# A hybrid decoder step: chunks of a half wait in the order for products sent, L in two buffers, X filled by memsets

## The chip, the cores and the metric

One core of a Trainium2 chip runs the whole step as one program. The metric is the time of one execution on the device, in microseconds. The engines of the core work side by side, each in the order in which its instructions were written out: TensorE (PE, with its weight loads PEld), VectorE (DVE), ScalarE (ACT), GpSimd (POOL) and SyncE (SP), which here only issues DMAs. POOL issues DMAs too.

## The reference

A layer of a decoder for 1024 tokens of a prompt and 8 samples of 4 tokens (T = 1056 columns). A wide projection feeds a causal convolution branch and an RWKV-7 branch, and two gates merge them; a gated MLP with a short convolution follows.

```python
h = rmsnorm(x, norm_mix_g)
z = h @ w_in                     # conv | r, k, v, lora | gates
u = zc[..., :D_CONV] * jax.nn.sigmoid(zc[..., D_CONV:])
c, new_conv = causal_dwconv(conv_buf, u, conv_dw_w, conv_dw_b)
ya = jax.nn.silu(layernorm(c, ...)) @ w_conv_out
# RWKV-7: S_t = S_{t-1} diag(w_t) + (S_{t-1} a_t) b_t^T + v_t k_t^T ;  y_t = S_t r_t
yh, new_wkv = wkv7_scan(wkv_state, rh, decay, kh, -kk, kk * ah, vh)
yb = ((groupnorm(yh) + bonus) * gout) @ w_rw_out
m = gates[..., :D_MODEL] * ya + gates[..., D_MODEL:] * yb
x = x + m @ w_mix_out
up = rmsnorm(x, norm_ffn_g) @ w_up
cu, new_ffn = causal_dwconv(ffn_buf, up, ffn_dw_w, ffn_dw_b)
x = x + (jax.nn.gelu(cu[..., :D_FF]) * cu[..., D_FF:]) @ w_down
```

## The kernel before

Every large product is done with split operands: a weight tile of 128 columns is loaded (`wraw`), rounded on ACT (`whi`, L48) and its rest taken on DVE (`wlo`, L49), and three matmuls (high by high, high by low, low by high) of 352 columns are summed in PSUM (tile `mm`, written at L54). A tile of 128 output rows is 3 blocks of 8 x 3 = 72 such matmuls.

`mixer_a` does the convolution input, the LoRA parts and the first six tiles of k, r and v. `mixer_b` does the recurrence and, between its steps, other products. The recurrence is cut into 16 halves n of 4 heads and 256 tokens (J = n // 4 counts the group of heads, n % 4 the place in the sequence). Each half goes through:

- `prep` and `operands`: loads k, r, v and others from DRAM, scales them, writes E and BK. A half of group J needs the k, r and v tiles 2J and 2J + 1 (`s_prep` waits for "rkv").
- `stage`: products of BK and E, whose PSUM tiles DVE evicts into LQ (L1024, L1028); the diagonal blocks of 32 go to DRAM (`dL`, L1038) and come back as `L` with one lane per partition, four times over (L1040). A triangular **solve** on DVE follows: `X` is set to the identity (L1043), and 31 pairs of a multiplication into `tm` (L1047) and an addition into `X` (L1049) build the inverse. `X` goes to DRAM (`dX`, L1051) and back into LQ (L1055).
- `combine`: two transposes on DVE (L1085) and 32 small matmuls complete the inverse.
- `chain`: 4 chunks of 64 tokens, one after the other, since each needs the state that the one before leaves. A chunk has three steps of four matmuls into a tile `c`; after each DVE (and ACT) must answer: `R0` (L1143), `UV` (L1151), `UV` or `Sf` (L1162). ACT takes the result out of tile `y` at the end (`Yev`, L1173).
- `group_norm`, and beside it the samples' work (`s_samples`) and the layer norm of the convolution (`s_ln`).

Other products stand between: 18 tiles of k, r and v (`rkv_tile`, j from 2 to 7), 16 gates (`gate`) and 8 tiles of the convolution's output (`conv_out`, 36 matmuls each). They come from the generator `fillers`. The loop `drive` writes the program: it holds a clock that counts matmul columns, takes a step of the first stream whose time has come, and one filler matmul group when none has. A stream that waits for something undone looks again every 400 units. So this loop sets in which order work is written; the tile framework then orders each engine's instructions once more by its own plan. In `fillers`, k, r and v tiles come first; then gates as far as `due` allows: the first GATE0 = 5 freely, and gate number g + 5 only when chain g is written. `conv_out` waits for the last chain and for `ln`; its input tile lies where the halves' E, BK, LQ and UV lay (`conv_in`). Behind it come `merge`, `mix` and the MLP (`tail`).

Of the kernel before, what the change touches and what calls it, by code (L numbers as in the profile page):

```python
# [31 lines left out]
class Net:  # L32
# [587 lines left out]
    def wkv_consts(self):  # L620
        nc, cp = self.nc, self.cp

        self.mb = cp.tile([128, 8, 32], F32, name="mb")
        nc.vector.memset(self.mb, 0.0)
        self.mrow = cp.tile([128, 8], F32, name="mrow")
        self.ms = cp.tile([128, 2, 32], F32, name="ms")
        nc.vector.memset(self.mrow, 1.0)
        nc.vector.memset(self.ms, 1.0)
        for b in range(8):
            nc.vector.memset(self.mb[:, b, 4 * b:4 * b + 4], 1.0)  # L630
        for p in range(4):
            r = self.mrow[32 * p:32 * (p + 1)]

            nc.gpsimd.affine_select(out=r, in_=r, pattern=[[-4, 8]], compare_op=ALU.is_ge, fill=0.0, base=0, channel_multiplier=1)
            nc.gpsimd.affine_select(out=r, in_=r, pattern=[[4, 8]], compare_op=ALU.is_ge, fill=0.0, base=3, channel_multiplier=-1)
            m = self.ms[32 * p:32 * (p + 1)]
            for q in range(2):
                x = m[:, q]
                nc.gpsimd.affine_select(out=x, in_=x, pattern=[[1, 32]], compare_op=ALU.is_ge, fill=0.0,
                                        base=-1 + q, channel_multiplier=-1)  # L640
                nc.gpsimd.tensor_tensor(
                    out=x.rearrange("p (b t) -> p b t", t=4), in0=x.rearrange("p (b t) -> p b t", t=4),
                    in1=r.rearrange("p (b o) -> p b o", o=1).to_broadcast([32, 8, 4]), op=ALU.mult)

        self.x0 = cp.tile([128, 8, 32], F32, name="x0")
        nc.vector.memset(self.x0, 0.0)
        for q in range(4):
            x = self.x0[32 * q:32 * (q + 1)]
            nc.gpsimd.affine_select(out=x, in_=x, pattern=[[4, 8], [-1, 32]], compare_op=ALU.not_equal, fill=1.0,
                                    base=q, channel_multiplier=0)  # L650

        self.tri = cp.tile([128, 2, 64], F32, name="tri")
        nc.vector.memset(self.tri, 1.0)
        for x in range(2):
            w = self.tri[64 * x:64 * x + 64]
            nc.gpsimd.affine_select(out=w, in_=w, pattern=[[1, 2], [1, 64]], compare_op=ALU.is_ge, fill=0.0,
                                    base=-1, channel_multiplier=-1)
        self.bt = cp.tile([128, 128], F32, name="bt")
        nc.vector.memset(self.bt, 0.0)
# [21 lines left out]
    def mixer_b(self):  # L681
        nc, a = self.nc, self.a
        self.wkv_consts()
        self.t2_left = self.T2N
        self.want = 0
        self.t_stage = {}
        self.st, self.pr, self.ch = {}, {}, {}
        with ExitStack() as e:
            self.t4 = self.pool(e, "t4b", 3)
            self.t2 = self.pool(e, "t2", self.T2N)  # L690
            self.e_sg = ExitStack()
            self.sg = self.pool(self.e_sg, "stage", 3, side="right")
            self.ln = self.pool(e, "lanes", 1)
            self.sm = self.pool(e, "small", 2)
            sp = self.pool(e, "samples")
            self.sG, self.sQK = (sp.tile([128, 4, 64], F32, name=x) for x in ("sG", "sQK"))
            self.sbv = sp.tile([128, 4, 32], F32, name="sbv")
            self.sUV = sp.tile([128, 8, 64], F32, name="sUV")
            self.sPC = sp.tile([128, 8, 8], F32, name="sPC")
            dram = lambda nm, m, w: [self.dr.tile([m, w], F32, name=f"{nm}{i}") for i in range(ND)]  # L700
            self.d_BT, self.d_S = dram("d_BT", 64, 128), dram("d_S", 128, 512)
            self.d_bv = [self.dr.tile([128, 2, TP], F32, name=f"d_bv{i}") for i in range(ND // 2)]
            self.drive([self.s_chain(), self.s_comb(), self.s_stage(), self.s_norm(), self.s_prep(), self.s_samples(), self.s_ln(), self.s_y(), self.s_shift()],
                       self.fillers())
            self.e_sg.close()
# [44 lines left out]
    def s_chain(self):  # L750
        for n in range(self.NH):
            yield from self.wait(("comb", n))
            yield from self.chain(n)
            self.done.add(("chain", n))

# [23 lines left out]
    def s_prep(self):  # L779
        for n in range(self.NH):  # L780
            k = [("rkv", j, x) for j in (n // 4 * 2, n // 4 * 2 + 1) for x in range(3)]
            if n == 8 + self.SQ[2]:
                k.append(("steps", 0))
            yield from self.wait(*k)
            yield from self.take(8, 2)
            yield from self.prep(n)
            yield from self.wait(*([("chain", n - 3)] if n > 2 else []))
            self.operands(n)
            self.done.add(("prep", n))

    def s_samples(self):
        def one(g, n):
            yield from self.take(n)
            yield from g
            self.t2_left += n
        for g in range(2):
            for j in range(4 * g, 4 * g + 4):
                yield from self.wait(("prep", j // 2 * 4 + self.SQ[j // 2]))
                yield from one(self.samples_in(j), 4)
                if g:  # L800
                    yield from one(self.samples_state(j - 4), 3)
            yield from one(self.samples_steps(4 * g), 4)
            self.done.add(("steps", g))
        for j in range(4, 8):
            yield from one(self.samples_state(j), 3)
# [47 lines left out]
            self.t2_left += 1  # L853
            yield 5000

    GATE0 = 5

    def fillers(self):
        gates = [(i, x) for x in range(2) for i in range(ND)]
        due = lambda: len(gates) > 2 * ND - self.GATE0 or ("chain", 2 * ND - len(gates) - self.GATE0) in self.done  # L860
        tiles = [(j, x) for j in range(2, ND) for x in range(3)]
        conv = list(range(ND))
        loaded = False
        while gates or tiles or conv:
            if not loaded and ("chain", self.NH - 1) in self.done and "ln" in self.done:
                self.conv_in()
                loaded = True
            if tiles:
                yield from self.rkv_tile(*tiles.pop(0))
            elif gates and due():  # L870
                yield from self.gate(*gates.pop(0))
                if not gates:
                    self.done.add("gates")
            elif conv and loaded:
                yield from self.conv_out(conv.pop(0))
            else:
                yield 1
# [17 lines left out]
    def prep(self, n):  # L895
# [32 lines left out]
        nc.scalar.activation(out=t1, in_=kn, func=AF.Square)  # L928
        hs = [slice(0, 64), slice(64, 128)]
        if smp:  # L930
            ARs = self.sm.tile([128, 2, 2, 32], F32, tag="ARs", name="ARs")
            BKs = self.sm.tile([128, 2, 2, 32], F32, tag="BKs", name="BKs")
            vs = self.sm.tile([128, 2, 32], F32, tag="vs", name="vs")
            bt4 = lambda t: t.rearrange("p u (b t) -> p u b t", t=4)
            nc.gpsimd.tensor_tensor(out=bt4(ARs[:, :, 0]), in0=sp(kn), in1=PS_[:, :, :, 0:4], op=ALU.mult)
            nc.gpsimd.tensor_tensor(out=bt4(ARs[:, :, 1]), in0=sp(r), in1=PS_[:, :, :, 1:5], op=ALU.mult)
            nc.gpsimd.tensor_copy(out=vs, in_=v[:, :, 256:288])
# [73 lines left out]
    def stage(self, n):  # L1011
# [24 lines left out]
        for x in range(2):  # L1036
            for d in range(2):
                nc.sync.dma_start(out=dL[x, d].rearrange("c i j -> i c j"), in_=LQ[64 * x + 32 * d:64 * x + 32 * d + 32, :, 32 * d:32 * d + 32])  # L1038
        L = self.ln.tile([128, 32, 32], F32, tag="L", name="L")
        nc.sync.dma_start(out=L, in_=dL.rearrange("(o h) d c i j -> o (h d c) (i j)", o=1).to_broadcast([4, 32, 1024]))  # L1040
        X = self.ln.tile([128, 8, 32], F32, tag="X", name="X")
        tm = self.ln.tile([128, 80], F32, tag="tm", name="tm")
        nc.vector.tensor_copy(out=X, in_=self.x0)  # L1043
        for s in range(31):
            a, m = s // 4 + 1, 31 - s
            tp = tm[:, :a * m].rearrange("p (a m) -> p a m", m=m)
            nc.vector.tensor_tensor(out=tp, in0=L[:, s:s + 1, s + 1:32].to_broadcast([128, a, m]),  # L1047
                                    in1=X[:, :a, s:s + 1].to_broadcast([128, a, m]), op=ALU.mult)
            nc.vector.tensor_tensor(out=X[:, :a, s + 1:32], in0=X[:, :a, s + 1:32], in1=tp, op=ALU.add)  # L1049
        for q in range(4):  # L1050
# [650 lines left out]
```

## Time and profile before

| | |
|---|---|
| median of 3 runs | 2529.82 us (2526.34 to 2546.9) |
| the profiled execution | 2521.95 us, span 2520.3 us |
| mean granted clock of TensorE | 0.928 of 2.4 GHz |
| PE busy | 2341.8 us (93%) |
| DVE busy | 1646.8 us (65%) |
| ACT busy | 877.9 us (35%) |
| POOL busy | 263.2 us (10%) |
| DMA | 230.65 MB, mean 92 GB/s |

The span is the profiled execution from its first instruction to its last. A share of busy time is an average over stages with different limits; a busy PE is not a PE at its peak, since ends of matmuls are modelled. The granted clock has two levels, 1.2 and 2.4 GHz, and a number between them is a mean over a stretch.

### The profile page before, as it was taken

What the parts mean: (1) busy time and instruction counts of PE and PEld (TensorE: products, weight loads), DVE (VectorE), ACT (ScalarE), POOL (GpSimd) and SP (SyncE); (2) the same over time, 40 slices, a digit from 0 to 9 for tenths busy, and PEclk for the clock granted to TensorE, in tenths of its full rate; (3) what the DMA queues carried; (4) which work ended last, traced back from release to release, by engine and by line L of the source; (5) the groups of instructions that cost most, each with busy time, mean ns of one, the idle gap of its engine ahead of it and who ended that gap; (6) DMA issues with size and microseconds to landing.
All of it is one profiled execution on the core that took longest, in us unless ns stands there. A gap on an engine that the chain in (4) does not pass through costs nothing.

```text
span 2520.3 us, 41895 instructions
## 1 busy us (share of the span) xinstructions
PE 2341.8 (93%) x16094; PEld 2114.6 (84%) x16094; DVE 1646.8 (65%) x4190; ACT 877.9 (35%) x1748; POOL 263.2 (10%) x562
## 2 busy tenths in 40 slices
PE   6789998987889689889999999999999999999998
PEld 5778886765668567767879999999999999999998
DVE  5999777688787877786862344475555545545556
ACT  4234333344344433543443222333232322223235
POOL 2313311011111111221221100000000000000000
PEclk9989997867679789897999999999999999999999
DMA  4124543243323332434334654431111111111111
GB/s 124 49 75 147 172 131 98 55 108 86 107 58 100 107 106 78 125 85 107 106 83 148 234 167 132 122 125 44 46 41 54 35 51 46 45 48 44 51 52 70
DMA packets 289295, 230.65 MB, mean 92 GB/s; under 512 B 82333, under 2 KB 265271, under 8 KB 288575
## 3 DMA queue, kind: packets, MB, share of 16 engines
q1 hardware_dynamic: 268615, 170.17, 24.3%
q0 software_dynamic: 20480, 57.80, 6.6%
q8 instruction: 127, 2.08, 0.4%
q14 instruction: 73, 0.60, 0.1%
HBM read 157.45 MB, written 70.45 MB: 90 GB/s over the span
## 4 chain that ended last, share of the span: by engine, by line
PE 78%; DVE 12%; DMA 6%; ACT 2%; issue 2%; SPq 1%; DVEq 0%; ACTq 0%; POOLq 0%
PE mm L54 62%; PE w L54 6%; PE c L54 2%; PE y L54 2%; DMA L<-dL 2%; DVE sg L359 2%; PE w L61 2%; DMA dX<-X 2%; DVE X L1049 1%; DVE tm L1047 1%; DVE wlo L49 1%; DMA d_ma<-ga 0%; SPq L1051 0%; DVE E L1030 0%; DVE UV L1162 0%
## 5 line engine op out<-in xcount | busy, mean ns | idle before, releaser
L54 PE MATMUL mm<-hH,whi 128*128 128x352 f32 (+1 forms) x2568 | 875.9, 341 | 14.1 <-DVE bcol L497 12.7
L54 PE MATMUL mm<-hH,wlo 128*128 128x352 f32 (+1 forms) x2568 | 851.9, 333 | 18.6 <-DVE wlo L49 18.6
L54 PE MATMUL mm<-hL,whi 128*128 128x352 f32 (+1 forms) x2568 | 854.2, 333 | 0.2 <-DVE hL L248 0.2
L54 PEld LDWEIGHTS mm<-hH,whi 128*128 128x128 f32 (+1 forms) x2568 | 491.2, 191 | 42.8 <-DVE bcol L497 14.3
L54 PEld LDWEIGHTS mm<-hH,wlo 128*128 128x128 f32 (+1 forms) x2568 | 491.6, 192 | 30.8 <-DVE wlo L49 20.8
L54 PEld LDWEIGHTS mm<-hL,whi 128*128 128x128 f32 (+1 forms) x2568 | 492.6, 192 | 11.0 <-issue 2.2
L48 ACT ACTIVATE whi<-wraw 128x1024 fp32r<-128x1024 f32 (+2 forms) x123 | 126.1, 1025 | 425.6 <-PE mm L54 340.3
L1533 DVE TENSOR_TENSOR u<-mm,rs 128x352 f32<-128x352 f32 x144 | 73.5, 511 | 225.1 <-PE mm L54 225.0
L49 DVE TENSOR_TENSOR wlo<-wraw,whi 128x1024 fp32r<-128x1024 f32 (+2 forms) x123 | 145.4, 1182 | 91.5 <-ACT whi L48 91.4
L359 DVE SCALAR_TENSOR_TENSOR sg<-cu,par,sg 128x1024 f32<-128x1024 f32 x120 | 165.4, 1382 | 1.5
L54 PE MATMUL mm<-fH,whi 128*128 128x352 f32 x504 | 163.4, 324 | 0.0
L54 PE MATMUL mm<-fH,wlo 128*128 128x352 f32 x504 | 162.8, 323 | 0.0
L54 PE MATMUL mm<-fL,whi 128*128 128x352 f32 x504 | 162.7, 323 | 0.0
L1588 DVE TENSOR_TENSOR acc<-mm,acc 128x352 f32<-128x352 f32 x168 | 86.9, 522 | 93.6 <-PE mm L54 93.6
L1563 DVE SCALAR_TENSOR_TENSOR c<-u,par,c 128x1024 f32<-128x1024 f32 x96 | 122.9, 1280 | 7.7 <-ACT c L1559 5.3
L54 PE MATMUL w<-E,BK 64*128 64x128 f32 x512 | 93.2, 332 | 32.4 <-DVE tm L1047 13.1
L54 PEld LDWEIGHTS w<-E,BK 64*128 64x128 f32 x512 | 76.5, 227 | 49.4 <-issue 27.3
L1047 DVE TENSOR_TENSOR tm<-L,X 128x60 f32<-128x60 f32 (+24 forms) x496 | 100.4, 202 | 23.6 <-DMA L<-dL 18.4
L1049 DVE TENSOR_TENSOR X<-X,tm 128x60 f32<-128x60 f32 (+24 forms) x496 | 100.4, 202 | 5.3
L54 PEld LDWEIGHTS mm<-fH,whi 128*128 128x128 f32 x504 | 94.8, 188 | 0.5
L54 PEld LDWEIGHTS mm<-fH,wlo 128*128 128x128 f32 x504 | 95.0, 188 | 0.0
L1122 ACT ACTIVATE SP<-UV,PC 64x64 f32<-64x64 f32 x192 | 64.3, 343 | 87.9 <-DVE UV L1162 78.0
(404 smaller groups left out, 3663.5 us busy)
## 6 DMA issues: line engine op xcount, KB each, us to landing
wraw<-w_in SPq DMA_DIRECT2D x50, 512.0 KB
wraw<-w_up SPq DMA_DIRECT2D x48, 512.0 KB
wraw<-w_down SPq DMA_DIRECT2D x32, 384.0 KB
L<-dL SPq DMA_DIRECT2D x16, 512.0 KB
d_alr<-la POOLq DMA_DIRECT2D x8, 528.0 KB, 3.2
d_cum<-lc POOLq DMA_DIRECT2D x8, 528.0 KB, 3.5
d_gout<-lg POOLq DMA_DIRECT2D x8, 528.0 KB, 4.0
d_k<-k POOLq DMA_DIRECT2D x24, 176.0 KB, 2.9
```

The lines of the kernel that those rows point to most:

```text
L48: nc.scalar.activation(out=hi[:, :nk, :m], in_=raw[:, :nk, :m], func=AF.Copy)
L49: (lo_eng or nc.vector).tensor_tensor(out=lo[:, :nk, :m], in0=raw[:, :nk, :m], in1=hi[:, :nk, :m].bitcast(F32), op=ALU.subtract)
L54: self.nc.tensor.matmul(out, l, r, start=start, stop=stop)
L61: self.nc.tensor.transpose(out, x, ident)
L359: nc.vector.scalar_tensor_tensor(out=c[:, 0:TP], in0=u[:, t:t + TP], scalar=self.col("conv_w", t * 4 + i), in1=c[:, 0:TP], op0=ALU.mult, o ...
L1047: nc.vector.tensor_tensor(out=tp, in0=L[:, s:s + 1, s + 1:32].to_broadcast([128, a, m]), in1=X[:, :a, s:s + 1].to_broadcast([128, a, m]), ...
L1049: nc.vector.tensor_tensor(out=X[:, :a, s + 1:32], in0=X[:, :a, s + 1:32], in1=tp, op=ALU.add)
L1122: nc.scalar.activation(out=at(SP, u, x), in_=src(x)[:, u], func=AF.Copy, scale=PC[hs[x], 4 * u + c:4 * u + c + 1])
L1533: nc.vector.tensor_tensor(out=u[:, 2 + t0:2 + t0 + m], in0=p, in1=rs[:, t0:t0 + m], op=ALU.mult)
L1563: nc.vector.scalar_tensor_tensor(out=c[:, 0:TP], in0=u[:, t:t + TP], scalar=wt, in1=c[:, 0:TP], op0=ALU.mult, op1=ALU.add)
L1588: nc.vector.tensor_tensor(out=acc[i][:, s], in0=ps[:, :BW], in1=acc[i][:, s], op=ALU.add)
```

## The change

Five edits go together:

1. `s_chain` counts: before half n's chain is written, 4 + 2n filler tiles (at most 34, which is all 18 of k, r and v and all 16 gates) must have been written. `fillers` counts them in `filled`.
2. GATE0 is 16, so gates wait for no chain.
3. `L` (one buffer of 4 KB a partition) is replaced by `LT` (rows 0 to 15 of the block, 2 KB) and `LB` (the lower right quarter, 1 KB), each with two buffers. LT comes in one DMA, LB in four.
4. `X` is set by five memsets on POOL instead of a copy on DVE from a constant `x0`, which is dropped.
5. `ARs`, `BKs` and `vs` have one buffer instead of two, and the `prep` that writes them waits for the samples of the group before ("samples").

```diff
-        self.x0 = cp.tile([128, 8, 32], F32, name="x0")
...
     def s_chain(self):
         for n in range(self.NH):
             yield from self.wait(("comb", n))
+            while self.filled < min(self.FILL[0] + self.FILL[1] * n, 34):
+                yield self.POLL
             yield from self.chain(n)
...
+            if n // 4 and n % 4 == self.SQ[n // 4]:
+                k.append(("samples", 2 * (n // 4) - 1))
...
                 yield from one(self.samples_in(j), 4)
+                self.done.add(("samples", j))
...
-    GATE0 = 5
+    GATE0 = 16
+    FILL = (4, 2.0)
...
             if tiles:
                 yield from self.rkv_tile(*tiles.pop(0))
+                self.filled += 1
             elif gates and due():
                 yield from self.gate(*gates.pop(0))
+                self.filled += 1
...
-            ARs = self.sm.tile([128, 2, 2, 32], F32, tag="ARs", name="ARs")
+            ARs = self.sm.tile([128, 2, 2, 32], F32, tag="ARs", name="ARs", bufs=1)
...
-        L = self.ln.tile([128, 32, 32], F32, tag="L", name="L")
-        nc.sync.dma_start(out=L, in_=dL.rearrange("(o h) d c i j -> o (h d c) (i j)", o=1).to_broadcast([4, 32, 1024]))
+
+        LT = self.ln.tile([128, 16, 32], F32, tag="LT", name="LT", bufs=2)
+        LB = self.ln.tile([128, 16, 16], F32, tag="LB", name="LB", bufs=2)
+        lanes = dL.rearrange("h d c i j -> (h d c) i j")
+        nc.sync.dma_start(out=LT, in_=lanes[:, 0:16].rearrange("(o l) i j -> o l (i j)", o=1).to_broadcast([4, 32, 512]))
+        for q in range(4):
+            nc.sync.dma_start(out=LB[32 * q:32 * q + 32], in_=lanes[:, 16:32, 16:32])
         X = self.ln.tile([128, 8, 32], F32, tag="X", name="X")
         tm = self.ln.tile([128, 80], F32, tag="tm", name="tm")
-        nc.vector.tensor_copy(out=X, in_=self.x0)
+        nc.gpsimd.memset(X, 0.0)
+        for q in range(4):
+            nc.gpsimd.memset(X[32 * q:32 * q + 32].rearrange("p a t -> p (a t)")[:, q:256:36], 1.0)
         for s in range(31):
             a, m = s // 4 + 1, 31 - s
             tp = tm[:, :a * m].rearrange("p (a m) -> p a m", m=m)
-            nc.vector.tensor_tensor(out=tp, in0=L[:, s:s + 1, s + 1:32].to_broadcast([128, a, m]),
+            nc.vector.tensor_tensor(out=tp, in0=(LT[:, s:s + 1, s + 1:32] if s < 16 else LB[:, s - 16:s - 15, s - 15:16]).to_broadcast([128, a, m]),
                                     in1=X[:, :a, s:s + 1].to_broadcast([128, a, m]), op=ALU.mult)
```

What edits 1 and 2 do to the engines' order shows at the last chain. On PE before, this piece is from the last half's chain (`c` and `y` are its matmuls, `mm<-hH` and `mm<-hL` those of a gate):

```order
L54 MATMUL c<-R_13195,LQ 64x64 x4
L54 MATMUL mm<-hH,wlo 128x352
L54 MATMUL mm<-hH,whi 128x352
L54 MATMUL mm<-hL,whi 128x352
L54 MATMUL y<-UV,LQ 64x64
L54 MATMUL mm<-hH,wlo 128x352
L54 MATMUL c<-UV,BK 64x64 x4
L54 MATMUL y<-UV,LQ 64x64 x3
```

After the change, the end of the last chain on PE, up to the first matmul of `conv_out` (`mm<-csH`):

```order
L54 MATMUL c<-R_14305,LQ 64x64 x4
L54 MATMUL y<-UV,LQ 64x64
L54 MATMUL c<-UV,BK 64x64 x4
L54 MATMUL y<-UV,LQ 64x64 x3
L61 MATMUL w<-ident,Sf 64x128 x2
L54 MATMUL mm<-csH,whi 128x352
L54 MATMUL mm<-csL,whi 128x352
```

The products of gates that stood between the steps, and those that followed the chain, now stand ahead of it, between the steps of earlier chains.

On DVE before, the start of half 9's solve: `X<-x` sets X, `tm<-L,X` and `X<-X,tm` are the solve, and `LQ<-w` are evictions of half 10's stage, from which half 10's L is made:

```order
L1043 COPY X<-x_2805 128x256
L1024 TENSOR_TENSOR LQ<-w,nin 64x4x64
L1028 TENSOR_TENSOR LQ<-w,tri 64x4x64
L1030 TENSOR_TENSOR E_8806<-w,tri 64x512
L1047 TENSOR_TENSOR tm<-L,X 128x31
L1024 TENSOR_TENSOR LQ<-w,nin 64x4x64
L1049 TENSOR_TENSOR X<-X,tm 128x31
L1028 TENSOR_TENSOR LQ<-w,tri 64x4x64
L1047 TENSOR_TENSOR tm<-L,X 128x30
```

After the change, evictions of half 9's stage on DVE, between the solves of halves 8 and 9; the first multiplication of half 9's solve stands 24 rows behind the last of these rows:

```order
L1026 TENSOR_TENSOR LQ<-w,nin 64x4x64
L669 SCALAR_TENSOR_TENSOR ry<-rt,ry 128x8
L1030 TENSOR_TENSOR LQ<-w,tri 64x4x64
L1251 TENSOR_TENSOR Yev<-Yev,ry 128x512
L1032 TENSOR_TENSOR E_8681<-w,tri 64x512
L941 TENSOR_TENSOR alr<-alr,k 128x576
L1026 TENSOR_TENSOR LQ<-w,nin 64x4x64
L1030 TENSOR_TENSOR LQ<-w,tri 64x4x64
L1032 TENSOR_TENSOR E_8682<-w,tri 64x512
```

The stage's evictions moved from within the solve before to behind it, and the copy into X is gone from DVE. X is set on POOL now, here between the memsets of the same stage's LQ:

```order
L1197 DMA out_p_wkv<-so 64x4x64
L1029 MEMSET LQ 32x4x32 x2
L1050 MEMSET X 128x256
L1052 MEMSET X 32x8 x4
L1029 MEMSET LQ 32x4x32
L506 DMA d_r_485<-r 128x352
```

The two rows that write X were added; before, the memsets of LQ and the DMA issues stood without them.

## Rows read from the trace of the kernel before

**Rows 1.** Page, chain that ended last: shares of the span by engine.
```profile
PE 78%; DVE 12%; DMA 6%; ACT 2%; issue 2%; SPq 1%; DVEq 0%; ACTq 0%; POOLq 0%
```

**Rows 2.** Stretches: length, busy of PE, PEld, DVE, ACT, POOL (instructions), clock, DMA, GB/s.
```profile
1453.00:2520.00 1067.00, 1059.22 (x6595) 1040.23 (x6594) 578.45 (x998) 314.17 (x541) 21.50 (x81) 1.00 0.23 68
...
340.00:1321.00 981.00, 858.99 (x7034) 686.86 (x7033) 740.31 (x2710) 392.49 (x922) 137.22 (x301) 0.83 0.35 93
...
1321.00:1453.00 132.00, 127.70 (x792) 126.54 (x790) 45.54 (x72) 37.56 (x56) 16.41 (x30) 0.99 0.59 194
...
567.00:767.00 200.00, 160.82 (x1403) 128.75 (x1402) 162.91 (x644) 79.79 (x193) 21.38 (x48) 0.72 0.32 88
767.00:855.00 88.00, 81.60 (x715) 66.27 (x713) 63.37 (x197) 44.41 (x103) 11.39 (x25) 0.98 0.35 103
...
1092.00:1280.00 188.00, 176.98 (x1478) 139.20 (x1479) 144.18 (x531) 73.27 (x176) 38.33 (x76) 0.90 0.38 104
...
1197.00:1323.00 126.00, 125.53 (x1175) 97.99 (x1175) 90.62 (x335) 55.72 (x132) 26.01 (x46) 1.00 0.36 94
...
1280.00:1321.00 41.00, 41.00 (x392) 30.27 (x393) 21.36 (x63) 17.70 (x42) 6.01 (x10) 1.00 0.27 65
```

**Rows 3.** Stretches, the solve's additions (L1049) alone: length, DVE busy (instructions), clock.
```profile
767.00:855.00 88.00, 0.00 (x0) 0.98 0.35 103
...
1052.00:1092.00 40.00, 0.00 (x0) 0.89 0.47 116
```

**Rows 4.** Stretches, tile mm alone: length, busy of PE, PEld, DVE, ACT, clock.
```profile
340.00:1321.00 981.00, 428.41 (x1839) 317.41 (x1840) 40.53 (x134) 39.94 (x77) 0.83 0.35 93
567.00:767.00 200.00, 61.32 (x255) 47.56 (x256) 8.37 (x28) 5.54 (x10) 0.72 0.32 88
767.00:855.00 88.00, 53.36 (x249) 39.33 (x247) 7.23 (x24) 6.08 (x11) 0.98 0.35 103
1092.00:1280.00 188.00, 95.39 (x411) 68.39 (x412) 0.00 (x0) 8.24 (x18) 0.90 0.38 104
1197.00:1323.00 126.00, 76.65 (x336) 53.16 (x337) 0.00 (x0) 6.48 (x14) 1.00 0.36 94
1321.00:1453.00 132.00, 126.68 (x778) 125.29 (x778) 11.83 (x24) 9.60 (x21) 0.99 0.59 194
1333.00:1401.00 68.00, 68.00 (x430) 68.00 (x428) 0.00 (x0) 8.25 (x18) 1.00 0.35 106
```

**Rows 5.** Waits of DVE, 340 to 1321 us: total, times, longest.
```profile
DVE R L1143 <- PE c L54: 41.6, 29, 5.5
...
DVE tm L1047 <- DMA L<-dL: 18.4, 6, 6.1
```

**Rows 6.** Timeline of DVE: start, duration, line, operation; half 0's solve ends, 1's begins.
```profile
405.81 0.15 DVE L1049 TENSOR_TENSOR X<-X,tm 128x8 f32<-128x8 f32 x1
...
413.09 1.22 DVE L49 TENSOR_TENSOR wlo<-wraw,whi 128x1024 fp32r<-128x1024 f32 x1
414.22 0.28 DVE L1043 COPY X<-x 128x256 f32<-128x256 f32 x1
...
418.54 0.19 DVE L1047 TENSOR_TENSOR tm<-L,X 128x31 f32<-128x31 f32 x1 [0.71 <-DMA L<-dL]
```

**Rows 7.** Chain that ended last, behind the last half: start, duration, work.
```profile
1321.14 4.98 DMA cs<-d_cs
...
1331.82 66.18 PE mm L54 x416
```

**Rows 8.** Chain that ended last: landings of L and of dX.
```profile
408.04 10.41 DMA L<-dL
...
509.85 8.69 DMA dX<-X
```

**Rows 9.** Groups of POOL, 340 to 1321 us: busy, mean ns, idle before and its enders.
```profile
L1027 POOL MEMSET LQ<- 32x128 f32 x64 | 12.7, 199 | 179.0 <-DVE LQ L1024 158.1 <-DVE tm L1047 14.0 <-issue 5.3
```

**Rows 10.** Timeline of SP: start, duration, four issues of dX.
```profile
405.99 2.00 SPq L1051 DMA_DIRECT2D dX<-X  x4
```

More of the change, by code (lines that the diff above doesn't have):

```diff
@@ L643, in wkv_consts @@
                     in1=r.rearrange("p (b o) -> p b o", o=1).to_broadcast([32, 8, 4]), op=ALU.mult)
-        self.x0 = cp.tile([128, 8, 32], F32, name="x0")
[L646 to L650, printed above, removed]
         self.tri = cp.tile([128, 2, 64], F32, name="tri")
@@ L686, in mixer_b @@
         self.t_stage = {}
+        self.filled = 0
         self.st, self.pr, self.ch = {}, {}, {}
@@ L930, in prep @@
         if smp:
-            ARs = self.sm.tile([128, 2, 2, 32], F32, tag="ARs", name="ARs")
-            BKs = self.sm.tile([128, 2, 2, 32], F32, tag="BKs", name="BKs")
-            vs = self.sm.tile([128, 2, 32], F32, tag="vs", name="vs")
+            ARs = self.sm.tile([128, 2, 2, 32], F32, tag="ARs", name="ARs", bufs=1)
+            BKs = self.sm.tile([128, 2, 2, 32], F32, tag="BKs", name="BKs", bufs=1)
+            vs = self.sm.tile([128, 2, 32], F32, tag="vs", name="vs", bufs=1)
             bt4 = lambda t: t.rearrange("p u (b t) -> p u b t", t=4)
```

## Prediction

> **What bounds the kernel now.** I read the chain that ended last first: PE holds 78% of it, DVE 12%, DMA 6% [rows 1]. So TensorE's order decides, and the question is where it is not dense. The windows answer that [rows 2]: from 1453 us on PE is busy 1059.22 of 1067 us at clock 1.00, and nothing can be won there. The mixer's second half, from 340 to 1321 us (the 16 halves with their solves and chains), takes 981 us with PE busy 858.99, DVE 740.31 and a mean clock of 0.83. It is followed by 132 us (1321 to 1453) that are dense again.
>
> Three things are wrong with the 981 us. First, they hold only 1839 of the products named mm, while 778 more stand behind them [rows 4]; 8 conv tiles of 36 make 288 of those, so 490 gate products (6.8 tiles of 72) run alone after the last chain. Second, no half is solved in two stretches, 767 to 855 us and 1052 to 1092 us: the count of the solve's additions there is zero [rows 3]. An ordinary turn from one solve to the next took 12.7 us (405.81 to 418.54) [rows 6], so 88 + 40 - 2 x 12.7 = 103 us are lost. Halves 8 and 12 need k, r and v tiles that the order sends late: before, chains run ahead of them and then wait. Third, the clock follows the density of products: 255 of them in 200 us go with clock 0.72, 411 in 188 us with 0.90, 249 in 88 us with 0.98 [rows 2, 4].
>
> **What one matmul costs.** A dense stretch gives 68.00 us / 430 = 0.158 us for a product [rows 4]. From 1197 to 1323 us PE is busy 125.53 of 126 us at clock 1.00 with 336 products among 1175 matmuls [rows 2, 4]; the other 839 (chains, stages, transposes) are then worth (126 - 336 x 0.158) / 839 = 0.087 us each. At these prices the 981 us hold 1839 x 0.158 + 5195 x 0.087 = 742 us of work: PE is used to 0.76. The last stretch of four solves, 1092 to 1280 us, holds 411 products and 1067 others, 158 of 188 us: 0.84. The stretch 767 to 855 holds 249 and 466: 80 of 88 us, 0.91.
>
> **The order (GATE0, FILL), the stage.** After the change all 34 tiles stand before the end of the last chain, 1839 + 490 = 2329 products in the stage, two tiles ahead of each half; the last tile that half 8 needs is the 12th and that of half 12 the 18th, which chains 4 and 7 already wait for, and the two empty stretches have no reason left. The order also moves the solves: on DVE the rows between the last row of a solve and the first step of its own chain grow from a mean of 50 to 162 (over all 16), so a chain no longer waits for the transfers between them. PE work becomes 2329 x 0.158 + 5195 x 0.087 = 820 us. Below that the stage can't go; at the 0.84 of the last stretch it takes 976 us. DVE gains 7 splits of weights, 740.31 + 7 x 1.22 = 749 us (a split took 1.22 us) [rows 2, 6]; at the 0.815 of its densest stretch (162.91 of 200 us) [rows 2] it needs 919 us. I take 915 us, where PE would be used to 0.90, between the two stretches above: **-66 us**, with ends -5 and -161.
>
> **The last chain runs bare.** In the new order no product stands between its steps; what hid its latency is gone. Today the end, 1280 to 1321 us, is 41 us at clock 1.00 with PE full [rows 2]. By the prices, the matmuls alone are cheaper without the products, but a chain step waits for DVE and back (DVE waited 41.6 us in 29 times for the first product of a chunk, longest 5.5) [rows 5]. Between nothing and 15 us more than PE's use allows for, I take **+8 us**.
>
> **Behind the chain.** The 490 products leave: 132 us shrink to what remains. conv_in must wait for the chain's buffers, and after it 1331.82 - 1321.14 = 10.7 us pass until PE goes on with products that need it not; the load, the split and the subtraction end about there [rows 7]. Gates cover this today; then it is open. Conv keeps what lies between the end of the run of gates and the merge, 1453 - (1331.82 + 66.18) = 55 us, its stalls included. So 132 becomes 66: **-66 us**.
>
> **L, X.** Waits for the load of L cost DVE 18.4 us in 6 times, 3.1 us each [rows 5]. Two buffers let the load start earlier, but the new order sends stage evictions later: fewer than 35 DVE rows lie between a stage's last eviction and the first product of its solve in 11 halves, where 4 had so few. L landed in 10.41 us [rows 8], LT has half its bytes (5.2 us), LB comes as four DMAs of 32 KB in rows of 64 B; the nearest row, dX with four DMAs of 32 KB in rows of 128 B, took 8.69 us [rows 8]. So LT and LB take from 5 us to 5.2 + 2 x 8.69 = 22.6 us together; near L's own 10, I leave the single wait at 3.1 us: 11 x 3.1 - 18.4 = **+16 us** (ends -18 and 16 x 12 = +190). X by five memsets on POOL replaces a copy of 0.28 us on DVE [rows 6]; POOL is busy 137.22 of 981 us [rows 2], its memsets took 0.2 us [rows 9], and in the order X is filled between LQ's memsets of the same stage, so before the last eviction from which L is made: nothing. LQ's 64 memsets waited 158.1 us for DVE evictions [rows 9]; if the fill ended such a wait on the path, it would cost 2.5 us a half, 40 us in all. SP issues 64 DMAs more, four of them in 2.00 us by dX's [rows 10], while the solve before still runs: nothing, and 16 x 2 = 32 us if that cover is gone. Single buffers for ARs, BKs, vs and the wait for "samples" act once per four halves and the order has them long done: nothing.
>
> **Sum.** -66 + 8 - 66 + 16 = -108 us on the profiled execution's 2521.95 us: 2414 us. The median of the runs shown (2529.82) lies 8 us above that execution, which makes 2422 us; I say 2420.
>
> **Rivals.**
>
> *The stage gets no denser than its last stretch* (chance 0.20): 976 us, PE at 0.84. For it: in-order engines wait on each other at 0.72 to 0.90 clock today, even where 411 products stood in. -5 + 8 - 66 + 16 = -47: 2475 us, 2483 beside the median.
>
> *PE or DVE become truly dense* (0.10): DVE at 0.86 instead of 0.815 makes 871 us, and L's waits vanish: 749 / 0.86 - 981 + 8 - 66 = -168: 2354 us, 2362 beside the median. For it: the stretch from 1197 us has PE full at clock 1.00 with DVE at 90.62 of 126.
>
> *The products cost their whole price inside* (0.10, slower): PE takes matmuls in order, and each product that stands before a chain step delays it. If the empty stretches come back in other places and 490 products add between 0.158 us and today's mean of 428.41 / 1839 = 0.233 us [rows 4], the stage grows by 77 to 114 us; with +8, +16 and -66 that is +35 to +72 us, 2565 to 2602 us beside the median. It decides from (25 + 42) / 490 = 0.137 us for each. Against it: PE idles 122 of 981 us, and halves 8 and 12 waited for just these products.
>
> *LB's small rows* (0.04, slower): each solve starts t us later on DVE; without an L term the sum is -124, so it is slower by over 1% from t = (124 + 25) / 16 = 9.3 us on. At t = 12, L's unknown above: 2522 - 124 + 192 + 8 = 2598 us. Against it: the longest wait for L is 6.1 us [rows 5], and the second buffer lets LB start while a solve runs.
>
> By the Trainium skill (DMA: Bandwidth & Descriptors, Specifications) pieces under 512 B fall short of the line rate. If a row of 64 B cost as much as one of 512 B, LB would take as long as 1 MB at L's rate, some 21 us (an estimate), and the rival's t would be reached; no trace here has rows of 64 B.
>
> *No change* (0.04): the stage grows to some 1023 us and eats what the part behind it gives back (-66 + 8 + 16); this lies between the loose stage and the slow one and needs 0.80 of PE.
>
> **Numbers.** The forecast has 0.52, and the rivals what stands beside them. The range, 2355 to 2495 us, goes from the dense case to past the loose one and leaves out the slower ones and part of the fast one. A measurement of this kernel tells about 1% (25 us) from no change; faster by more than that: 0.52 + 0.20 + 0.10 = 0.82; the same 0.04 and the 0.02 of the slow rival that end just above no change, 0.06; slower 0.08 + 0.04 = 0.12.
>
> **What the profile of after would show.** Right: solves at an even pace with no stretch of 80 us without one; granted clock over 0.9 in the stage; the last Y of a chain (1321 us today) near 1321 - 66 + 8 + 16 = 1279 us, no gate product behind it, merge some 63 us later; FFN unchanged. L's waits on DVE near 34 us. Wrong if the stage ends at 1321 us or later, if DVE waits for LT or LB over 100 us, or if X is waited for on POOL.

## The result and the profile after

The kernel after takes 2422.07 us (median of 4 runs, 2415.14 to 2433.34), the kernel before 2530.69 us in the same comparison: a ratio of 0.9558, with a 95% interval from 0.9523 to 0.9593. The forecast was 2420 us. The profiled execution is the longest of the four (span 2431.6 us, mean clock 0.946; the other three have 2413.4 to 2421.5 us at 0.950 to 0.954), so the two spans differ by 88.7 us and the medians by 108.6. One execution of the kernel with two products a gate, 2641.71 us long, is a slow one and counts in no median or ratio below.

The windows of after, all engines (columns as in [rows 2]: length, busy of PE, PEld, DVE, ACT, POOL with their instructions, clock, DMA share, GB/s):

```profile
340.00:1305.00 965.00, 899.13 (x7535) 740.47 (x7534) 756.52 (x2716) 416.74 (x960) 159.93 (x399) 0.89 0.39 104
940.00:1240.00 300.00, 298.15 (x2648) 242.66 (x2647) 229.86 (x803) 133.28 (x318) 62.59 (x146) 0.95 0.42 111
1280.00:1305.00 25.00, 15.67 (x167) 11.90 (x165) 18.32 (x38) 15.08 (x29) 0.54 (x1) 0.61 0.39 152
1305.00:1365.00 60.00, 51.06 (x304) 48.92 (x301) 28.41 (x57) 15.49 (x22) 4.39 (x8) 0.91 0.74 233
1365.00:2431.00 1066.00, 1059.41 (x6594) 1040.20 (x6594) 578.85 (x998) 313.46 (x539) 21.59 (x81) 1.00 0.23 68
```

The stage now ends at 1305 us instead of 1321 [rows 2], and 60 us instead of 132 lie between it and the dense end, which has kept its 1066 us. So of the 88.7 us, some 72 come from behind the last chain and only 16 from the stage. The same stretches for the tile mm alone:

```profile
340.00:1305.00 965.00, 508.57 (x2332) 389.45 (x2331) 40.49 (x134) 49.66 (x98) 0.89 0.39 104
1305.00:1365.00 60.00, 49.12 (x288) 47.47 (x288) 11.38 (x24) 0.00 (x0) 0.91 0.74 233
```

All gate products are in the stage: 2332 products against 1839 [rows 4], and the 288 of the convolution alone behind it. The stretches that held no addition of a solve [rows 3] hold some now, and no more than 31.6 us lie between two solves anywhere (L1058 is the line of the additions; length, DVE busy, clock):

```profile
767.00:855.00 88.00, 8.14 (x41) 0.93 0.36 94
1052.00:1092.00 40.00, 5.07 (x24) 0.81 0.26 74
```

DVE's waits from 340 to 1305 us (total, times, longest): the wait for L's load is nearly gone, against 18.4 us in [rows 5].

```profile
DVE R L1152 <- PE c L54: 32.2, 30, 3.6
...
DVE tm L1056 <- DMA LT<-dL: 2.5, 3, 1.2
```

### The profile page after: what moved, and what is told of

It reads as the page before. It is cut to its first block, busy times and chain, and to the rows that moved or that the text cites. A ratio compares the mean times of both kernels' runs of the same rounds, so it can differ in the third digit from the quotient of the medians.

```text
span 2431.6 us, 42062 instructions
## 1 busy us (share of the span) xinstructions
PE 2305.7 (95%) x16094; PEld 2091.4 (86%) x16094; DVE 1642.9 (68%) x4175; ACT 878.5 (36%) x1750; POOL 269.8 (11%) x636
## 4 chain that ended last, share of the span: by engine, by line
PE 68%; DVE 6%; DMA 2%; ACT 2%; issue 1%; SPq 0%; POOL 0%; DVEq 0%; ACTq 0%; POOLq 0%
PE mm L54 55%; PE w L54 5%; PE c L54 3%; PE y L54 3%; PE w L61 2%; DMA d_ma<-ga 1%; DMA ga<-d_ga 1%; DVE Sf L1171 0%; DMA alr<-d_alr 0%; DVE X L1058 0%; DVE tm L1056 0%; ACT y L1219 0%; PE w L1451 0%; PE w L1536 0%; DVE BK L1003 0%
## 5 line engine op out<-in xcount | busy, mean ns | idle before, releaser
L54 PE MATMUL mm<-hH,wlo 128*128 128x352 f32 (+1 forms) x2568 | 850.3, 332 | 11.3 <-DVE wlo L49 11.3
L1058 DVE TENSOR_TENSOR X<-X,tm 128x60 f32<-128x60 f32 (+24 forms) x496 | 101.3, 204 | 5.6
L54 PE MATMUL w<-E,BK 64*128 64x128 f32 x512 | 83.1, 312 | 19.6 <-DVE BK L1004 10.9
L54 PEld LDWEIGHTS w<-E,BK 64*128 64x128 f32 x512 | 70.6, 213 | 34.4 <-issue 17.7
L54 PEld LDWEIGHTS mm<-fL,whi 128*128 128x128 f32 x504 | 94.9, 188 | 0.0
```

The costliest lines, as they stand in the source:

```text
L54: self.nc.tensor.matmul(out, l, r, start=start, stop=stop)
```

## The experiments

The theory at the outset: the order (edits 1 and 2) carries the gain, by the gates moved into the stage and by the vanished stretches without a solve; L and X are worth no more than the waits that DVE shows. The main rival: the new load of L (edit 3) carries a good part.

The table sums up all runs (each ratio against the kernel before on the same chip). "Last chain" is the end of its last product Y and "last conv" the start of the last product of conv_out, both from the trace of the profiled execution; from the first product of `mix` to the end it takes 974 to 975 us in every run.

| kernel | median us | ratio, 95% interval | last chain | last conv |
|---|---|---|---|---|
| before | 2530.69 | | 1321 | 1452 |
| after | 2422.07 | 0.9558 [0.9523, 0.9593] | 1305 | 1363 |
| order alone | 2487.17 | 0.9811 [0.9755, 0.9868] | 1343 | 1401 |
| L, X and buffers alone | 2503.21 | 0.9872 [0.9845, 0.9900] | 1294 | 1437 |
| LT, LB one buffer each | 2433.95 | 0.9601 [0.9560, 0.9643] | 1304 | 1362 |
| cap at 28 tiles | 2426.08 | 0.9583 [0.9541, 0.9625] | 1285 | 1347 |
| order, X on POOL | 2505.66 | 0.9866 [0.9822, 0.9909] | 1378 | 1436 |
| order, split load | 2434.77 | 0.9593 [0.9557, 0.9630] | 1301 | 1358 |
| cap at 18 tiles | 2457.03 | 0.9691 [0.9644, 0.9739] | 1286 | 1387 |
| two products a gate | 2441.01 | 0.9601 [0.9545, 0.9657] | 1310 | 1367 |
| order, L by four loads | 2481.26 | 0.9791 [0.9749, 0.9833] | 1344 | 1402 |
| LT by four loads | 2433.12 | 0.9601 [0.9578, 0.9624] | 1303 | 1363 |
| FILL (8, 1.6) | 2462.21 | 0.9711 [0.9685, 0.9736] | 1336 | 1394 |
| FILL (2, 2.0) | 2443.34 | 0.9670 [0.9640, 0.9700] | 1306 | 1368 |

### The order alone

The kernel before with edits 1 and 2.

```diff
+            while self.filled < min(self.FILL[0] + self.FILL[1] * n, 34):
+                yield self.POLL
...
-    GATE0 = 5
+    GATE0 = 16
+    FILL = (4, 2.0)
```

> The kernel before with edits 1 and 2 alone (the count, FILL, GATE0); L, X and the small buffers as before. Theory, the order carries it: only the waits for the load of L are missing, which fell from 18.4 us to 2.5 us between the two profiles, so 2420 to 2440 us. Rival, edits 3 to 5 carry half of the 108 us: about 2475 us. Rival, the new order needs the second buffer: DVE waits for L at 11 solves or more, 3.1 us and above each, so 2450 us or more and a wait of DVE for L of 34 us or more.

2487 us: 48 us less than before, not 90 or more. The theory falls. The stage, all engines and then the tile mm alone, in the trace of the order alone:

```profile
340.00:1342.00 1002.00, 909.57 (x7519) 745.70 (x7518) 757.55 (x2726) 416.16 (x959) 147.64 (x321) 0.88 0.37 102
```

```profile
340.00:1342.00 1002.00, 515.45 (x2330) 394.13 (x2329) 40.33 (x134) 49.55 (x98) 0.88 0.37 102
```

The order makes the stage longer, 1002 us against 981, and it holds 491 more products (0.044 us each, if they alone lengthen it); its gain is the 73 us behind the last chain. DVE's wait for L grew (here from 340 to 1342 us; columns as above):

```profile
DVE tm L1053 <- DMA L<-dL: 28.1, 9, 6.1
DVE X L1049 <- DMA dX<-X: 6.6, 3, 2.5
```

GATE0 does nothing: written with GATE0 = 5 or 16, the kernel before is the same program, and so are the order alone and after. The count (edit 1) makes the new order by itself.

### Edits 3 to 5 alone

The kernel after in the old order.

```diff
-    GATE0 = 16
-    FILL = (4, 2.0)
+    GATE0 = 5
+    FILL = (0, 0.0)
```

> The kernel after with FILL at (0, 0) and GATE0 at 5: edits 3 to 5 in the old order. Theory, the order carries it: within 1% of before, 2510 to 2535 us, with the two stretches without a solve still there and DVE's wait for L between 0 and 18 us. Rival, edits 3 to 5 carry half: about 2475 us.

2503 us, 32 us less than before, between the two expectations: edits 3 to 5 are worth something without the order. The stage ends at 1294 us instead of 1321, though both stretches without a solve are still there (87.7 and 39.7 us). Windows of this kernel for the solve's additions, then for all engines:

```profile
749.00:837.00 88.00, 0.00 (x1) 1.00 0.34 99
```

```profile
749.00:837.00 88.00, 86.17 (x728) 69.28 (x727) 62.37 (x197) 43.80 (x102) 12.40 (x31) 1.00 0.34 99
```

While no solve runs, PE is busy 86.17 of 88 us at clock 1.00. So little of PE's time was lost in that stretch. Which of edits 3 to 5 gives the 32 us is not shown here: before, DVE also waited for `dX` ahead of the copy into X (340 to 1320 us: total, times, longest), and this run changes L and X together.

```profile
DVE X L1043 <- DMA dX<-X: 15.0, 6, 3.7
```

### One buffer, X on POOL, the split alone

Three kernels between the order alone and after. First, after with one buffer each:

```diff
-        LT = self.ln.tile([128, 16, 32], F32, tag="LT", name="LT", bufs=2)
-        LB = self.ln.tile([128, 16, 16], F32, tag="LB", name="LB", bufs=2)
+        LT = self.ln.tile([128, 16, 32], F32, tag="LT", name="LT", bufs=1)
+        LB = self.ln.tile([128, 16, 16], F32, tag="LB", name="LB", bufs=1)
```

> The kernel after with one buffer each for LT and LB instead of two. If the second buffer took away the wait for L: DVE waits for LT or LB 16 to 35 us in total, 2430 to 2445 us. If the smaller load or the new place of the evictions did: DVE waits under 6 us, and the time is that of after, 2412 to 2432 us.

2434 us; DVE waits 5.2 us for LT in the trace from 340 to 1320 us. The two measures point to different sides, and the interval overlaps that of after, so the second buffer is worth 12 us or nothing; this stays open. Next, after with L whole:

```diff
-        LT = self.ln.tile([128, 16, 32], F32, tag="LT", name="LT", bufs=2)
...
+        L = self.ln.tile([128, 32, 32], F32, tag="L", name="L")
+        nc.sync.dma_start(out=L, in_=dL.rearrange("(o h) d c i j -> o (h d c) (i j)", o=1).to_broadcast([4, 32, 1024]))
```

> The kernel after with L whole again (one load of 512 KB, one buffer); X stays on POOL, the new order stays. It stands between the order alone (2487 us) and one buffer each for LT and LB (2434 us). In the order alone DVE waited 28.1 us for L and 6.6 us for X. If the load of L carries those 53 us: still about 28 us of waits for L, 2470 to 2490 us. If the copy of X does, because everything behind it on DVE waits for dX: 2430 to 2450 us.

2506 us, no better than the order alone (the intervals overlap): moving X to POOL brings nothing by itself. And the order alone with nothing but the split:

```diff
-        L = self.ln.tile([128, 32, 32], F32, tag="L", name="L")
...
+        LT = self.ln.tile([128, 16, 32], F32, tag="LT", name="LT")
+        LB = self.ln.tile([128, 16, 16], F32, tag="LB", name="LB")
```

> The order alone with L split into LT and LB of one buffer each; X is copied on DVE as before. If the load of L carries the 53 us between the order alone (2487 us) and one buffer each with X on POOL (2434 us): DVE waits for LT under 8 us, 2430 to 2450 us. If the copy of X does: 2470 to 2490 us. If both must go together: both this run and the one with X on POOL above 2460 us.

2435 us. **The split load carries it:** 52 of the 65 us between the order alone and after, and no interval between this run, the one with one buffer and after stands apart. The three kernels with the new order and L whole (order alone, X on POOL, and four loads below) lie at 2481 to 2506 us, the four with the split (this one, one buffer, after, and LT by four loads below) at 2422 to 2435 us. The 52 us are more than the 28.1 us that DVE was seen to wait. The timeline shows the place. In the order alone, half 8 (start, duration, engine, line; the last eviction of the stage, the issue of L's load, the first step of the solve):

```profile
824.47 0.43 DVE L1034 TENSOR_TENSOR LQ<-w,tri 64x256 f32<-64x256 f32 x1
826.46 0.56 SPq L1046 DMA_DIRECT2D L<-dL  x1
...
837.45 0.19 DVE L1053 TENSOR_TENSOR tm<-L,X 128x31 f32<-128x31 f32 x1 [4.99 <-DMA L<-dL]
```

The same in after:

```profile
798.32 0.42 DVE L1030 TENSOR_TENSOR LQ<-w,tri 64x256 f32<-64x256 f32 x1
...
800.89 0.56 SPq L1045 DMA_DIRECT2D LT<-dL  x1
...
806.97 0.19 DVE L1056 TENSOR_TENSOR tm<-LT,X 128x31 f32<-128x31 f32 x1 [0.96 <-DMA LT<-dL]
```

From the issue to the first step it takes 11.0 us with L and 6.1 with LT; over halves 4 to 11 it is 9.7 to 11.7 us and 5.9 to 8.2. Part of it shows as a wait of DVE, the rest is covered by rows of other work placed there. In other halves of after the load is issued while the solve before still runs, and up to 39.5 us pass; over all 16 the mean is 12.7 us, against 11.3 in the order alone. From the last eviction to the first step, the mean over the 16 halves (start of the first `tm` less the end of the last `LQ<-w,tri`) fell from 26.7 us in before to 22.5 with edits 3 to 5, and from 19.3 with the order alone to 16.0 with the split and 15.9 in after.

### Faster loads

L whole and in one buffer, but by four loads:

```diff
-        nc.sync.dma_start(out=L, in_=dL.rearrange("(o h) d c i j -> o (h d c) (i j)", o=1).to_broadcast([4, 32, 1024]))
+        for q in range(4):
+            nc.sync.dma_start(out=L[32 * q:32 * q + 32], in_=dL.rearrange("h d c i j -> (h d c) i j"))
```

> The order alone (2487 us), with L whole in one buffer but loaded by four DMAs of 128 KB, one for each copy, instead of one broadcast of 512 KB. In the order alone 9 to 13 us pass in each half from the issue of L's load to the first step of the solve, with the split 6 to 8 us where the load is issued behind the solve before. Theory, the time of the load stands on the path of each half, and any faster load helps: some 4 us in 9 to 16 halves, 36 to 64 us, so 2425 to 2450 us. Rival, the split helps because LT comes free half way through a solve and not because it lands sooner: still 2475 to 2500 us.

2481 us, as the rival has it, but the run does not decide. DVE no longer waits for L at all, and yet 34.8 us lie in the mean between the last eviction and the first step, and 15.7 to 21.5 us between issue and first step in halves 4 to 11: the plan of the tile framework has put other rows of DVE there. So a wait that vanishes from the list need not be time won. For LT the same edit:

```diff
-        nc.sync.dma_start(out=LT, in_=lanes[:, 0:16].rearrange("(o l) i j -> o l (i j)", o=1).to_broadcast([4, 32, 512]))
+        for q in range(4):
+            nc.sync.dma_start(out=LT[32 * q:32 * q + 32], in_=lanes[:, 0:16])
```

> The kernel after with LT loaded by four DMAs of 64 KB instead of one broadcast of 256 KB. In after 5.7 to 8 us pass from the issue of LT's load to the first step where the load is issued behind the solve before. Theory, the load's time stands on the path: if four loads land in 4 us, 1 to 2 us in each half, 15 to 30 us less than after, 2392 to 2407 us. Rival, the issues (four of LB's took 2.34 us on SP) eat what the transfer gives back: 2412 to 2432 us.

2433 us, no gain. In half 8 the packets of LT took 1.9 us instead of 3.9, but the mean from eviction to first step is 18.1 us against 15.9. Whether the split helps by landing sooner, by coming free half way through the solve, or by the rows that the plan then places ahead of the solve, stays open: each edit of the load moves all three.

### What a product in the stage costs

The count capped at 18 tiles: no chain waits for a gate.

```diff
-            while self.filled < min(self.FILL[0] + self.FILL[1] * n, 34):
+            while self.filled < min(self.FILL[0] + self.FILL[1] * n, 18):
```

> The kernel after with the count capped at 18 tiles: chains wait for tiles of k, r and v as after, but no chain waits for a gate, so the order is that of after up to chain 7, and some six gates stand behind the last chain again. As the prediction has it, the vanished stretches without a solve pay and the gates in the stage cost: 2415 to 2440 us. Rival, the stretches were dense and worth nothing, and the gates pay because they cost little inside (from edits 3 to 5 alone to after the end of the last chain moved by only 10.5 us for 490 products): 425 products back behind the chain at 0.158 us are 67 us, less what they cost inside, 0.02 to 0.04 us each: 2465 to 2485 us.

2457 us, between the two expectations. The tile mm in its stage and behind it:

```profile
340.00:1285.00 945.00, 454.91 (x2020) 335.97 (x2020) 40.56 (x134) 43.94 (x85) 0.88 0.37 97
1285.00:1389.00 104.00, 98.14 (x599) 96.68 (x599) 12.04 (x24) 5.96 (x13) 0.98 0.68 224
```

Against after, 312 products stand behind the stage instead of in it; the stage is 19 us shorter (0.061 us a product) and the stretch behind it 44 us longer (0.14 us a product). So the order's gain has two parts: 46 us from edits 3 to 5 alone to this kernel (k, r and v sent evenly, no stretch without a solve over 32 us; 269 more products in the stage, which yet ends 9 us earlier), and 35 us from here to after, for the gates.

Next, after with one of the three products of each gate left out:

```diff
+                    self.mm(ps[:m, :BW], wh[:, k, :m], xh[:, k, s], k == 0, False)
+                    self.mm(ps[:m, :BW], wh[:, k, :m], xl[:, k, s], False, k == nk - 1)
+                    self.clock += BW / 2.4
```

> The kernel after with one of the three products of each gate left out (low weights by high input, 384 of 1152 matmuls), so the gates are less exact; the order's clock counts as before. If a product in the stage costs what it costs in a dense stretch: 384 x 0.158 = 61 us less, about 2361 us. If it only fills time in which TensorE would wait: no change, 2412 to 2432 us, or more, as the clock falls with the density. Halfway, 0.08 us each: about 2391 us.

2441 us: with 386 products less in the stage (1946 against 2332) the time is not shorter. The stretch that is densest in after, all engines and then the tile mm alone:

```profile
940.00:1240.00 300.00, 283.42 (x2418) 226.04 (x2414) 229.70 (x803) 135.55 (x320) 63.38 (x148) 0.86 0.43 114
```

```profile
940.00:1240.00 300.00, 125.04 (x571) 95.44 (x571) 0.00 (x0) 16.62 (x36) 0.86 0.43 114
```

In after the same stretch has clock 0.95 and 773 products:

```profile
940.00:1240.00 300.00, 170.66 (x773) 127.23 (x772) 0.00 (x0) 14.62 (x32) 0.95 0.42 111
```

With 202 fewer, PE is busy only 15 us less, and the clock is 0.86. The matmuls that are left take longer: those of the tiles `w` (stages and transposes) 109.80 us for 951, against 96.11 us for 1011 in after. That the steps of solves and chains then set the pace fits this, but is argued, not shown.

### The lead and the end of the order

The cap at 28 tiles leaves gates for the last chain:

```diff
-            while self.filled < min(self.FILL[0] + self.FILL[1] * n, 34):
+            while self.filled < min(self.FILL[0] + self.FILL[1] * n, 28):
```

> The kernel after with the count capped at 28 tiles instead of 34: chains 12 to 15 wait for 28 tiles and no more, so about four gates are left for the last chain and the stretch behind it. Theory, the bare end is a loss by itself: the 32 us from 1280 to 1312 us of after hold 17 us of PE work at a mean clock near 0.6; four gates of 72 products at 0.158 us are 45 us and fill them, so 10 to 20 us less than after, 2402 to 2412 us. Rival, the stage is bound by its own steps and the gates only shift: what leaves the stage shortens it by nothing, 2422 to 2440 us.

2426 us, the same as after. The stage ends 20 us earlier, and its last 39 us are full; then:

```profile
1246.00:1285.00 39.00, 39.00 (x370) 29.04 (x370) 17.63 (x58) 15.11 (x39) 2.87 (x5) 1.00 0.29 89
1285.00:1353.00 68.00, 53.03 (x314) 51.46 (x313) 39.40 (x69) 23.81 (x33) 5.45 (x10) 0.91 0.78 253
```

Behind the chain 68 us pass with 53.03 of PE, where after has 60 with 51.06. The last conv product starts 15 us earlier than in after's profile, but the medians do not tell the two apart: the bare last chain costs nothing that four runs can show.

More tiles ahead of the first chain and fewer for each later half:

```diff
-    FILL = (4, 2.0)
+    FILL = (8, 1.6)
```

> The kernel after with FILL (8, 1.6) instead of (4, 2.0): chain 0 waits for 8 tiles, chain 15 for 32. In after TensorE is busy 298 of 300 us from 940 to 1240 us, but 356 of 400 us at clocks of 0.76 to 0.88 from 340 to 740 us. Theory, products are free where TensorE is not dense and cost their price where it is: two to four tiles of 72 products (11.4 us each) taken out of the dense part give 10 to 35 us, 2387 to 2412 us. Rival, the first chains start later by what they wait for and every later half with them: 2425 to 2460 us.

2462 us; the rival holds. Windows of this kernel, the solve's additions, then all engines:

```profile
463.00:530.00 67.00, 0.17 (x1) 1.00 0.35 95
```

```profile
463.00:530.00 67.00, 66.78 (x529) 59.55 (x528) 42.55 (x133) 27.22 (x59) 8.80 (x23) 1.00 0.35 95
640.00:940.00 300.00, 268.67 (x2101) 217.64 (x2102) 228.38 (x850) 126.56 (x294) 48.58 (x116) 0.78 0.35 95
```

Chain 1 starts at 516 us instead of 473, and half 3 is solved 66 us after half 2. In that stretch PE is full, and by 640 us it has done 895 products (from 340 us on) against 665 in after. By 940 us that lead is down to 1445 against 1404, at a clock of 0.78 from 640 us on (0.89 in after), and the chains have stayed behind: chain 5 by 39 us, the end of the last one by 31. Two tiles less ahead of each chain:

```diff
-    FILL = (4, 2.0)
+    FILL = (2, 2.0)
```

> The kernel after with FILL (2, 2.0) instead of (4, 2.0): every chain waits for two tiles less, and two to three gates are left for the last chain. With FILL (8, 1.6) half 3 was solved 66 us after half 2, since the first chains came late. Theory, the lead at the start costs and the pace of two tiles for each half pays: the first chains start 10 to 20 us sooner and the last one is covered, 2400 to 2415 us. Rival, TensorE is dense from 940 us on and sets the end, so what starts sooner waits there: 2416 to 2430 us. If half 8 or 12 has to wait for k, r and v again: a stretch of 60 us or more without a solve, 2435 us or more.

2443 us, 21 us more than after, which none of the three expected: no stretch without a solve over 32 us, and a loss. Chain 1 starts 22 us earlier than in after, chain 5 13 us, and the last chain ends at the same time. The first part is thinner:

```profile
340.00:640.00 300.00, 264.76 (x2038) 217.61 (x2037) 235.57 (x877) 116.22 (x269) 38.81 (x113) 0.79 0.35 91
```

After has 0.84 and 272.03 us there. The chains that were free sooner waited later: chain 9 starts 9 us after that of after. Where the 21 us lie the two profiles do not show, as they differ by 7 us alone. Of all kernels run none is faster than after.

## Why the prediction was right, and where it was not

**The time** came out, 2422.07 us for 2420. **The terms** did not: two of the stage are wrong, and their errors cancel in part. On the profiled executions the sum is -88.7 us for -108; the rest of the agreement is that after's profiled execution lies 11 us above its median. So the number is luck, and of the mechanism only what stands behind the chain is borne out.

*The order in the stage, -66.* Failed. The profiles give +22 us (before to the order alone) and +11 (edits 3 to 5 alone to after), the bare last chain included. The step that failed is the 103 us that were "lost" in the two stretches without a solve. They were counted on DVE; PE was busy 81.60 of 88 us at clock 0.98 in the first [rows 2], and with edits 3 to 5 it was busy 86.17 of 88 at 1.00. In the second, before (length, PE, PEld, DVE, ACT, POOL, clock, DMA, GB/s):

```profile
1052.00:1092.00 40.00, 35.84 (x302) 29.48 (x302) 24.31 (x64) 19.03 (x44) 6.59 (x18) 0.89 0.47 116
```

When the stretches vanished, the time came back in the turns between other solves: these add up to 289.9 us in before (88.2 and 40.5 for the two stretches), 314.1 in the order alone and 278.0 in after (sum of the times from the last addition of a solve to the first step of the next). With k, r and v sent evenly and no gate waited for (cap at 18), the stage is 9 us shorter than with edits 3 to 5 alone, not 103, and holds 269 products more. What the order gives is denser products in about the same time.

*The loose stage.* With 2332 x 0.158 + 5203 x 0.087 = 821 us of work in 965, PE is used to 0.85, what the first rival took (0.84), not 0.90. Its total of 2483 us failed mainly by the term for L that it shared with the forecast.

*L, +16.* Failed, in sign and size: with edits 3 to 5 the stage ends 27 us earlier in the old order, and with the split alone 42 us earlier in the new one, where the medians fall by 52 us. The prediction priced L by the residue that DVE shows as a wait, 18.4 us in 6 times [rows 5], and left each wait as it was. The chain that ended last had more to say. Before, five loads of L stand on it between 340 and 1321 us, 52.3 us in sum, the one of [rows 8] and these (start, duration, work):

```profile
348.57 10.19 DMA L<-dL
...
844.01 10.90 DMA L<-dL
893.75 10.67 DMA L<-dL
...
1187.69 10.17 DMA L<-dL
```

In after a single load of LT is left on it:

```profile
800.89 5.99 DMA LT<-dL
```

The 27 to 42 us measured lie between the two figures, and neither is a price: with L by four loads no load of L stands on that chain or in DVE's waits, and the time is that of the order alone; with one buffer each 32.0 us of LT and LB stand on it, and the time is within the noise of after. By which mechanism the split gains its 52 us stays open. The 34 us of waits foretold for the new order are near what L whole has (28.1 us). That fewer rows hide the load there fits this, and also that edits 3 to 5 bring 65 us in the new order and 32 in the old; that it is why the order alone fell short is not shown.

*The last chain bare, +8.* Nothing measurable, by the cap at 28; the chain itself takes 25 us at PE 15.67 and clock 0.61.

*Behind the chain, -66.* Held: -73 by the last conv product (1452 to 1363, less the 16 that the chain ends earlier). The two stretches in it, 10.7 us open and 55 for conv, were 6 and 54: after the last Y, the chain of waits in after (start, duration, work):

```profile
1305.33 4.65 DMA cs<-d_cs
...
1313.17 3.49 PE mm L54 x11
...
1329.16 6.06 DMA ga<-d_ga
...
1365.40 9.64 PE mm L54 x59
```

The round trips of the gates' tiles (`ga`) stand in this chain now, beside a PE that is busy 51.06 of 60 us; this is a wait that the prediction did not name.

*X, SP's issues, small buffers: nothing.* X held in the new order (no gain without the split, none seen with it); in the old one it was not run by itself, and the 15.0 us of waits for `dX` were not priced. The others showed no wait.

*The rivals.* That products cost their whole price inside is refuted: 0.044 us (order alone), 0.061 (cap at 18 against after) and none (two products a gate), where it decided from 0.137. LB's small rows cost no wait: in half 8 of after, LT's packets (2 KB) were through 3.9 us and LB's (64 B) 4.9 us after their first. From 796 to 812 us packets have means of 10.6 ns (64 B), 30.1 ns (512 B) and 105 ns (2 KB). By the Trainium skill (DMA: Bandwidth & Descriptors, Specifications) pieces under 512 B fall short of the line rate; the trace agrees, 64 B cost three times as much for each byte as 2 KB, but such a row is not as dear as one of 512 B, which the rival's 21 us needed.

*The signs.* No stretch of 80 us without a solve, no gate behind the chain, the MLP unchanged: right. Clock above 0.9 in the stage: 0.89. End of the chain near 1279 us: 1305. Waits for L near 34 us: 2.5.

## What to carry to other kernels

A gap on one engine is lost time only if the engine that sets the end is idle in it: read the windows of that engine over the gap before pricing the gap's end. A load that each turn of a loop needs can be worth more than its waits in the list, which count only what the scheduler found no rows to cover (28.1 us listed, 52 gained), and a wait that vanishes can be worth nothing (L by four loads). Look for the load on the chain that ended last as well, and time the edit, since each one also moves other rows. And when a sum comes out right, undo its terms one by one: here the order was worth 48 us alone, the split load 52 on top of it, and the forecast had put everything on the first and a loss on the second.

## What was not expected of the hardware

Taking 386 products out of the stage gained nothing, and the granted clock from 940 to 1240 us was 0.86 instead of 0.95, a mean between the two levels of 1.2 and 2.4 GHz. Products added to this thin stage cost less than their dense price, here 0.0 to 0.06 us against 0.158, and taking them away gave as little. The differences between executions of one program go with the clock too: the four of the order alone took 2473, 2484, 2491 and 2506 us at mean clocks of 0.939, 0.934, 0.934 and 0.924.

Few packets of the broadcast load ran at once: in half 8 of after, LT's 128 packets of 2 KB add up to 13.5 us in 3.9 us of time, 3.4 at a time; as four loads they took 1.9 us, 8.4 at a time.
